# Rotating images by 180 degrees: a last load in two pieces, an earlier release of the first store, and wider copies

## The chip, the cores and the metric

The kernel runs on one core of a Trainium2 chip. Its time is the device time of one execution in microseconds (us); the kernel before takes 122.82 us, the median of three runs (122.74 to 122.94).

## The reference

The input is a batch of images in 32-bit floats, 32 x 3 pictures of 256 x 256. Every picture is turned by 180 degrees, which reverses its rows and the elements of each row:

```python
batch, c, h, w = 32, 3, 256, 256
return np.rot90(x, k=2, axes=(-2, -1)).astype(np.float32)
```

Seen as a flat list of 65,536 elements, a picture is simply reversed. There is no arithmetic: 25.17 MB are read, reordered and written back.

## The kernel before

The 96 pictures make three groups of 32 (G). Each picture is cut into four runs of E = 16,384 elements, so a group is a tile of 128 partitions with one run of 64 KB in each: 8.39 MB. The three groups have a tile of their own, A, Bt and Ct (lines 43 to 45), and all of them fit on the chip at once, beside a small spare tile T of J elements per partition (line 46).

A reversed picture needs its four runs in the opposite order, and each run reversed inside. The two halves of this work are done by different parts of the chip:

- `inside(t)` (line 60) reverses each partition's run in place on the vector engine, DVE. It takes a strip of J elements from the front and the strip of J that mirrors it at the back, and swaps them with three copies (line 52): the back strip reversed into T, the front strip reversed into the back, T into the front. With J = E // 16 = 1024 there are 8 such pairs, thus 24 copies of 128 x 1024 for a tile and 72 in all. They are kept in the order of the program.
- `store(t, g)` (line 58) writes the tile out with the four runs of each picture in the opposite order (`::-1` in the output's access pattern).

All loads (line 55) and stores are issued by the sync engine, SP, whose instructions go in order, and all go into one DMA queue (q1 in the profile) that feeds 16 DMA engines. Each transfer of a whole tile gives every DMA engine eight pieces of 64 KB, one for each of eight partitions, and then a 4-byte write to the transfer's semaphore. The transfer has landed when all 16 engines have done theirs.

SP's program has six transfers: load A, load Bt, load Ct, store A, store Bt, store Ct. The three loads wait for nothing. Store A waits for A to be turned and, by a dependency that is added by hand (line 74), for the last copy on Bt. Store Bt, behind it on SP, needs only the same copy, and store Ct needs the last copy on Ct. At the end SP waits for the landing of the three stores.

The order in the program is:

```python
inside(A)
last = inside(Bt)
first = store(A, 0)      # held back until `last` is done
store(Bt, 1)
inside(Ct)
store(Ct, 2)
```

Of the kernel before, what the change touches and what calls it, by code (L numbers as in the profile page):

```python
# [2 lines left out]

os.environ.setdefault("NEURON_RT_ULTRASERVER_MODE", "4")

# [4 lines left out]


@with_exitstack
def kernel(
    ctx: ExitStack,
    tc: tile.TileContext,
    x: bass.AP,
    out: bass.AP,
):

    nc = tc.nc
    P = 128

    B, C, H, W = x.shape
    L = H * W
    G = 32
    E = L // 4
    J = E // 16

    x4 = x.rearrange("b c h w -> (b c) (h w)").rearrange(
        "(g n) (s e) -> g (n s) e", n=G, s=4)
    o4 = out.rearrange("b c h w -> (b c) (h w)").rearrange(
        "(g n) (s e) -> g n s e", n=G, s=4)  # L40

    pool = ctx.enter_context(tc.tile_pool(name="slots", bufs=1))
    A = pool.tile([P, E], x.dtype, tag="A")
    Bt = pool.tile([P, E], x.dtype, tag="B")
    Ct = pool.tile([P, E], x.dtype, tag="C")
    T = pool.tile([P, J], x.dtype, tag="T")

    def back(t, lo, hi):
        return t[:, hi - 1:(lo - 1 if lo else None):-1]

    def copy(dst, src):
        return tc.keep_in_program_order(nc.vector.tensor_copy(out=dst, in_=src))  # L52

    def load(t, g, lo, hi):
        return nc.sync.dma_start(out=t[:, lo:hi], in_=x4[g][:, lo:hi])  # L55

    def store(t, g):
        return nc.sync.dma_start(out=o4[g][:, ::-1, :], in_=t[:, :])

    def inside(t):  # L60
        for lo in range(0, E // 2, J):
            hi = E - lo - J
            copy(T[:, :], back(t, hi, hi + J))
            copy(t[:, hi:hi + J], back(t, lo, lo + J))
            last = copy(t[:, lo:lo + J], T[:, :])
        return last

    load(A, 0, 0, E)
    load(Bt, 1, 0, E)
    load(Ct, 2, 0, E)  # L70
    inside(A)
    last = inside(Bt)
    first = store(A, 0)
    tc.add_manual_dep(
        first.ins, last.ins.name,
        mybir.DependencyInfo(mybir.DependencyClass.Sync, mybir.DependencyReason.DATA),
        reason="the first store is queued when the second group is turned")
    store(Bt, 1)
    inside(Ct)
    store(Ct, 2)  # L80


# [1 line left out]
_INS = ['x']  # L84
_OUTS = [((32, 3, 256, 256), 'float32')]


# [23 lines left out]
```

## Time and profile before

| what | value |
|---|---|
| time, median of 3 runs | 122.82 us (122.74 to 122.94) |
| profiled execution: its own time, and its span | 122.94 us, 121.16 us |
| bytes read and written | 25.17 MB and 25.17 MB |
| mean rate over the span | 415 GB/s |
| DVE busy | 50.0 us (41% of the span), 72 copies |
| one copy of 128 x 1024 | 694 ns |
| issue to landing: load A, load Bt, load Ct | 22.0, 40.9, 59.8 us |
| issue to landing: store A, store Bt, store Ct | 22.2, 40.8, 41.3 us |

The span is the time from the first to the last instruction on record; the 1.78 us between it and the execution's own time lie around it. "Issue to landing" counts from SP's instruction to the moment that the transfer's semaphore is complete, and so includes the time in which a transfer waits behind others in the queue. The DMA view counts the packets that start in a window; a packet is one piece of a transfer on one DMA engine, and packets under 512 bytes are the writes to semaphores. As a packet's bytes are counted where it starts, the rate in a short window can be far above or below the true one.

### The profile page before, as it was taken

To read this page: it belongs to the slowest core of one execution; us is meant where nothing else is said; L and a number is where in the kernel's file an instruction comes from. 1 tells how busy PE (TensorE), PEld (TensorE's weight loads), DVE (VectorE), ACT (ScalarE), POOL (GpSimd) and SP (SyncE) were. 2 spreads that over 40 slices of the span, in tenths; PEclk is the share of its full clock that TensorE was granted. 3 is DMA by queue.
4 is the path that set the end of the run, shared out by engine and by line. 5 is a ranking of instruction groups with operands and counts; after the bars stand their busy time and mean duration, and the time that the engine had idled before them with its cause. 6 is when DMAs were issued, how large, how long until landed. Compare 5 with 4: busy or idle time off the path is not lost.

```text
span 121.2 us, 126 instructions
## 1 busy us (share of the span) xinstructions
DVE 50.0 (41%) x72; POOL 0.2 (0%) x4
## 2 busy tenths in 40 slices
DVE  0000000499999399999669999900000000000000
POOL 0000000000000000000000000000000000000000
DMA  9778977997889877978898879887988798889880
GB/s 346 346 346 368 671 346 346 389 649 346 346 368 671 346 346 346 692 346 346 346 671 368 349 346 649 368 368 346 649 368 368 346 649 368 368 346 649 368 368 0
DMA packets 865, 50.34 MB, mean 415 GB/s; under 512 B 96, under 2 KB 96, under 8 KB 96
## 3 DMA queue, kind: packets, MB, share of 16 engines
q1 hardware_dynamic: 864, 50.33, 96.7%
q14 instruction: 1, 0.01, 0.0%
HBM read 25.17 MB, written 25.17 MB: 415 GB/s over the span
## 4 chain that ended last, share of the span: by engine, by line
DMA 34%; DVE 28%; another core or an unknown queue 2%; issue 1%; SPq 0%; DVEq 0%
DMA Bt<-in_x_dram 34%; DVE T L52 9%; DVE Ct L52 9%; DVE Bt L52 9%; SPq L55 0%; DVEq L52 0%
## 5 line engine op out<-in xcount | busy, mean ns | idle before, releaser
L52 DVE COPY T<-A 128x1024 f32<-128x1024 f32 x8 | 5.6, 694 | 23.0 <-DMA A<-in_x_dram 22.8
L52 DVE COPY T<-Ct 128x1024 f32<-128x1024 f32 x8 | 5.6, 694 | 2.2 <-DMA Ct<-in_x_dram 2.0
L52 DVE COPY T<-Bt 128x1024 f32<-128x1024 f32 x8 | 5.6, 694 | 2.2 <-DMA Bt<-in_x_dram 2.0
L52 DVE COPY A<-A 128x1024 f32<-128x1024 f32 x8 | 5.6, 694 | 0.3
L52 DVE COPY Ct<-Ct 128x1024 f32<-128x1024 f32 x8 | 5.6, 694 | 0.3
L52 DVE COPY Ct<-T 128x1024 f32<-128x1024 f32 x8 | 5.6, 694 | 0.3
L52 DVE COPY Bt<-T 128x1024 f32<-128x1024 f32 x8 | 5.5, 694 | 0.3
L52 DVE COPY Bt<-Bt 128x1024 f32<-128x1024 f32 x8 | 5.5, 694 | 0.3
L52 DVE COPY A<-T 128x1024 f32<-128x1024 f32 x8 | 5.5, 693 | 0.3
L95 POOL MEMSET const-uint8-127<- 128x1 uint8 x1 | 0.1, 103 | 0.0
L95 POOL MEMSET const-bfloat16-1.0<- 128x1 bf16 x1 | 0.1, 102 | 0.0
L95 POOL MEMSET const-float32-0.0<- 128x1 f32 x1 | 0.1, 99 | 0.2 <-issue 0.2
L95 POOL MEMSET const-float32-1.0<- 128x1 f32 x1 | 0.1, 99 | 0.0
## 6 DMA issues: line engine op xcount, KB each, us to landing
A<-in_x_dram SPq DMA_DIRECT2D x1, 22.0
Bt<-in_x_dram SPq DMA_DIRECT2D x1, 40.9
Ct<-in_x_dram SPq DMA_DIRECT2D x1, 59.8
out_dram<-A SPq DMA_DIRECT2D x1, 22.2
out_dram<-Bt SPq DMA_DIRECT2D x1, 40.8
out_dram<-Ct SPq DMA_DIRECT2D x1, 41.3
```

The lines of the kernel that those rows point to most:

```text
L52: return tc.keep_in_program_order(nc.vector.tensor_copy(out=dst, in_=src))
L95: nc = _bacc.Bacc("TRN2", target_bir_lowering=False, num_devices=1)
```

## The change

Three things are different:

1. The load of Ct is issued as two transfers: the first 14,592 elements of each partition (58,368 bytes, "the body"), and the last TAIL = 1,792 elements (7,168 bytes, "the tail"), which is 0.92 MB over the 128 partitions.
2. Store A no longer waits for the last copy on Bt. By hand it now waits for the landing of the body. Store Bt waits for Bt to be turned, and store Ct for Ct, as each needs. The first copy on Ct waits for both pieces of its load.
3. J is E // 8 = 2048 and not E // 16 = 1024, so that there are 12 copies of 128 x 2048 for a tile, 36 in all, and T has twice the size. The elements that are copied are the same number.

SP's program has seven transfers then, and the order of the transfers in the queue is load A, load Bt, body, tail, store A, store Bt, store Ct.

```diff
-    J = E // 16
+    J = E // 8
...
     def copy(dst, src):
-        return tc.keep_in_program_order(nc.vector.tensor_copy(out=dst, in_=src))
+        tc.keep_in_program_order(nc.vector.tensor_copy(out=dst, in_=src))
...
             copy(T[:, :], back(t, hi, hi + J))
             copy(t[:, hi:hi + J], back(t, lo, lo + J))
-            last = copy(t[:, lo:lo + J], T[:, :])
-        return last
+            copy(t[:, lo:lo + J], T[:, :])
 
+    TAIL = 1792
     load(A, 0, 0, E)
     load(Bt, 1, 0, E)
-    load(Ct, 2, 0, E)
+    body = load(Ct, 2, 0, E - TAIL)
+    load(Ct, 2, E - TAIL, E)
     inside(A)
-    last = inside(Bt)
     first = store(A, 0)
     tc.add_manual_dep(
-        first.ins, last.ins.name,
+        first.ins, body.ins.name,
         mybir.DependencyInfo(mybir.DependencyClass.Sync, mybir.DependencyReason.DATA),
...
-    store(Bt, 1)
-    inside(Ct)
-    store(Ct, 2)
+    for g, t in ((1, Bt), (2, Ct)):
+        inside(t)
+        store(t, g)
```

More of the change, by code (lines that the diff above doesn't have):

```diff
@@ L64, in inside @@
             copy(t[:, hi:hi + J], back(t, lo, lo + J))
-            last = copy(t[:, lo:lo + J], T[:, :])
-        return last
+            copy(t[:, lo:lo + J], T[:, :])
+    TAIL = 1792
     load(A, 0, 0, E)
     load(Bt, 1, 0, E)
-    load(Ct, 2, 0, E)
+    body = load(Ct, 2, 0, E - TAIL)
+    load(Ct, 2, E - TAIL, E)
     inside(A)
-    last = inside(Bt)
     first = store(A, 0)
     tc.add_manual_dep(
-        first.ins, last.ins.name,
+        first.ins, body.ins.name,
         mybir.DependencyInfo(mybir.DependencyClass.Sync, mybir.DependencyReason.DATA),
-        reason="the first store is queued when the second group is turned")
-    store(Bt, 1)
-    inside(Ct)
-    store(Ct, 2)
+        reason="the first store is queued while the last strip is on its way")
+    for g, t in ((1, Bt), (2, Ct)):
+        inside(t)
+        store(t, g)
 _INS = ['x']
```

## The prediction

> **What bounds the kernel now.** I read the page first: its slices of the DMA engines and its queues.
>
> ```profile
> DMA  9778977997889877978898879887988798889880
> q1 hardware_dynamic: 864, 50.33, 96.7%
> q14 instruction: 1, 0.01, 0.0%
> ```
>
> The queue that holds all loads and stores is busy for 96.7% of the span on all 16 engines. DVE (41%) is no bound. In the packet records a 64 KB packet takes 2.418 us and the next starts 2.414 us after it (2.419 us in the stores), so six transfers of eight packets cost an engine at least 48 x 2.414 = 115.9 us of the 121.16 us span. What a change can win is the other 5.3 us: the start, the place where loads give way to stores, and the engines that lag at the end. The page's chain of work is no help here; it stops at the last copy on Ct, some 40 us before the end.
>
> SP's own waits come next, then the timeline round 60 us.
>
> ```profile
> SPq L58 <- DVE Bt L52: 36.8, 1, 36.8
> SPq L106 <- DMA out_dram<-Ct: 19.2, 1, 19.2
> ```
>
> ```profile
> 58.91 0.69 DVE L52 COPY Bt<-T 128x1024 f32<-128x1024 f32 x1
> 59.63 0.63 SPq L58 DMA_DIRECT2D out_dram<-A  x1
> 60.30 0.59 SPq L58 DMA_DIRECT2D out_dram<-Bt  x1
> 61.57 0.70 DVE L52 COPY T<-Ct 128x1024 f32<-128x1024 f32 x1 [1.97 <-DMA Ct<-in_x_dram]
> ```
>
> Store A is issued at 59.63 us, as soon as Bt is turned. Is that early enough to follow the loads without a gap? The DMA view of 60.4 to 60.9 us, then of 60.9 to 61.3 us:
>
> ```profile
> DMA packets 15, 0.00 MB, mean 0 GB/s; under 512 B 15, under 2 KB 15, under 8 KB 15
> ...
> DMA packets 17, 1.05 MB, mean 2621 GB/s; under 512 B 1, under 2 KB 1, under 8 KB 1
> ```
>
> No. Fifteen engines write load Ct's semaphore between 60.54 and 60.84 us, and none has begun a store by 60.9 us. The 16 first packets of store A start from 60.906 us on, 1.28 us and more after the issue. In the packet records the engines stand idle for 0.07 to 0.49 us (mean 0.26 us). The sixteenth engine, 0.35 us behind since the first load, writes its semaphore at 61.18 us and idles for 0.10 us.
>
> The end: the windows 119 to 119.3 us and 119.3 to 120.5 us, and before them 68.5 to 68.9 us.
>
> ```profile
> DMA packets 3, 0.14 MB, mean 348 GB/s; under 512 B 0, under 2 KB 0, under 8 KB 0
> q1 hardware_dynamic: 2, 0.13, 81.1%
> q14 instruction: 1, 0.01, 4.8%
> ```
>
> ```profile
> DMA packets 14, 0.00 MB, mean 0 GB/s; under 512 B 14, under 2 KB 14, under 8 KB 14
> ...
> DMA packets 2, 0.00 MB, mean 0 GB/s; under 512 B 2, under 2 KB 2, under 8 KB 2
> ```
>
> Fourteen engines are done by 119.2 us. The late one of the border ends at 119.47 us, and another at 119.94 us. SP waits for that last one, wakes at 120.37 us, and the span ends 0.8 us later. This last engine was level with the rest at 65.8 us. Then its packet took 2.72 us, an 8 KB packet of the instruction queue (q14) held it for 0.30 us at 68.57 us, and the next took 2.77 us: together 0.95 us behind. So two engines decide the end: one that lost 0.95 us to an instruction fetch, and 0.47 us in front of it one that was late from the start.
>
> **The change part by part.** *Half as many copies.* J = 2048 removes 36 DVE instructions. The trace has no copy of 128x2048; its price lies between 0.694 us (nothing for width) and 1.388 us (twice the row). I take the upper end, as the data doubles. With the 0.034 us that the trace has between copies, a tile takes at most 12 x 1.42 = 17.1 us against 17.5 us. Bt, landed at 42.1 us, is turned by 59.2 us at the latest; store Bt comes behind store A and has 19 us of queue before it, so this hides. Ct is turned by 78.6 us, and store Ct's turn in the queue is at 99.7 us: 21 us of cover. As DVE work this edit is worth 0.
>
> It may do something else: move the fetch. At 68.57 us only DVE is executing; SP waits from 61.5 to 79.0 us, PE, ACT and POOL since 0.8 us. The fetch is DVE's by elimination. DVE was then at its 58th copy, some 63 instructions in. In the changed kernel it has 36 copies and about 42 instructions in all before the last store, so a fetch that comes with the instruction count doesn't occur while data moves. Bounds: 0 (the fetch is not tied to the count) to 0.95 us (all that its engine lost). The end gains only until the next engine decides, 119.94 - 119.47 = 0.47 us. I take 0.47 us.
>
> The Trainium skill ("Runtime: NRT & Kernel Launch", Instruction fetch mechanics) speaks against this: refills are blocks of 256 instructions that the sequencer streams ahead, their cost mostly hidden. The trace has one packet of 8 KB with 72 copies in the program, and an engine that lost 0.95 us beside it. By the page the fetch would be worth nothing, and the sum 122.8 us.
>
> *The release of store A.* It now waits for the body to land; A is turned at 40 us or earlier. The body is 58,368/65,536 of load Ct, so an engine ends it 7,168/65,536 x 19.3 = 2.11 us before it ends the whole load. The late engine counts: 61.18 - 2.11 = 59.07 us, and 0.3 us to landing (61.18 to 61.48 us in the trace) gives 59.37 us. SP's wait and the issue take about 0.09 us (at the start SP passes a wait at 0.65 us and issues at 0.73 us): store A goes out at 59.46 us and not 59.63 us, 0.17 us earlier. So the new wait replaces the old with little difference. At 1.28 to 1.40 us from issue to first packet, packets can start at 60.74 to 60.86 us, while engines finish the tail at 60.54 to 60.84 us. The mean idle falls from 0.26 to about 0.1 us; for the late engine, which decides, from 0.10 us to between 0 and 0.10. I take 0.05 us gained. Behind store A on SP waits only store Bt, issued 0.67 us later as now.
>
> *One more load.* SP issues four, 0.43 us for the fourth at 2.1 us; it hides behind 60 us of queue. DVE's first copy on Ct waits for both pieces, which end when the whole did. The rate of 7 KB pieces is not in the trace. From below: no cost, as the semaphore packets between queued transfers pass without a measurable gap; none can be gained, as the bytes are the same. From above: every new piece starts cold, as load A's first packet does (3.15 us median for 2.42), 0.73 us each and 8 x 0.73 = 5.8 us. The nearest row is the border of load A and load Bt inside a running queue, where 9 semaphore-size packets at 5 ns would be 0.04 us. I take 0.04 us.
>
> The Trainium skill ("DMA: Bandwidth & Descriptors", Anatomy of one DMA) charges each DMA about 2.0 us fixed beside its bytes, and its rules for kernel authors want 1 MiB or more in one DMA; the tail is under that. In the trace loads land 19.3 us apart, their bytes' time and no more. With a fixed 2.0 us exposed the sum would be 124.3 us.
>
> Sum against the profiled execution (122.94 us = span 121.16 + 1.78): -0.47 - 0.05 + 0.04 = -0.48, thus 122.46 us. That execution is 0.12 us above the median of 122.82, to which I apply the difference: 122.34, said as 122.3 us. A measurement of this kernel tells about 0.2% (0.25 us) from no change, so faster means below 122.57 and slower above 123.07 us.
>
> **The rivals.** *The fetch stays, or comes later under the stores* (same). What speaks for it: one packet is thin evidence for a trigger, and the removed instructions may only shift it. Against: DVE alone was running. Then the fetched engine still decides; store A's release gives it at most 0.17 us and the tail takes 0.04: 122.7 us, 122.6 to 122.9.
>
> *Nothing late remains* (faster). If the engine that lags by 0.35 us from its first packet is chance, the end falls to the 14 others: 119.94 - 119.19 = 0.75 us, with 0.17 us of closed gap: 121.9 to 122.0 us. Against: some engine always starts last, and 16 must land.
>
> *The short pieces are slow* (slower). The mechanism is that 7 KB rows don't stay in flight behind each other; place, the tail at 58.6 to 60.7 us; all engines pay. It decides beyond 0.48 + 0.25 = 0.73 us, 0.09 us for each of the eight, which is one cold start for the transfer. Two cold starts, at the tail and behind it, give 122.34 + 1.46 = 123.8 us; one gives 123.07. For it: a piece of this size isn't in the trace. Against: queued pieces show no gap, 4-byte ones included.
>
> **How the numbers follow.** The forecast case, 0.55: 122.1 to 122.55 us. Fetch stays, 0.20: same, except a tenth of it (0.02) at its fast end. Nothing late, 0.08. Short pieces slow, 0.17: 0.13 slower, 0.04 same because the price stays under the point of decision. Faster 0.55 + 0.08 + 0.02 = 0.65, same 0.22, slower 0.13. The range from 122.0 to 122.95 us holds the forecast, most of the fetch rival and the cheap end of the short pieces; outside are some 0.05 below and 0.14 above.
>
> **What the changed profile would show.** No q14 packet in the queues, or one on another place; the windows at the end with 15 engines within 0.2 us and one straggler, not two. Store A issued at 59.4 to 59.5 us and its first packets from 60.75 us. 128 packets of 7,168 bytes, eight of them in 2.1 to 2.2 us on an engine. Copies near 1.2 to 1.4 us. I am wrong if a q14 packet remains inside the stores and the last engine still ends 0.4 us behind, or if the loads end later than 61.3 us.

## The result and the profile after

The changed kernel takes 122.31 us (median of 6 runs, 122.04 to 122.44), the kernel before 122.78 us in the runs beside it. The ratio is 0.9956, with a 95% interval of 0.9941 to 0.9970: 0.47 us or 0.4% faster. Forecast were 122.3 us, and 122.0 to 122.95 us as the range.

The profiled execution of the changed kernel took 122.44 us with a span of 120.7 us, against 122.94 and 121.2 us before. The page's queues after the change (packets, MB, share of 16 engines):

```profile
DMA  9888988898889779799599888988898889888990
...
q1 hardware_dynamic: 1008, 50.33, 97.2%
```

There is no line for the instruction queue q14 any more; before, it had one packet of 8 KB. The 1008 packets are 864 and the 144 of the second piece of load Ct (128 of data, 16 for semaphores).

SP's and DVE's timeline round 60 us, and one row of the page's groups for the price of a copy:

```profile
55.88 1.23 DVE L52 COPY Bt<-T 128x2048 f32<-128x2048 f32 x1
59.63 0.63 SPq L58 DMA_DIRECT2D out_dram<-A  x1
60.36 0.55 SPq L58 DMA_DIRECT2D out_dram<-Bt  x1
61.82 1.23 DVE L52 COPY T<-Ct 128x2048 f32<-128x2048 f32 x1 [4.71 <-DMA Ct<-in_x_dram]
```

```profile
L52 DVE COPY Bt<-Bt 128x2048 f32<-128x2048 f32 x4 | 4.9, 1227 | 0.1
```

Bt is turned at 57.1 us, 2.5 us earlier than before. Store A nevertheless goes out at 59.63 us, to the hundredth as before, because now it waits for the body. The end, in the DMA view of 119 to 119.3 us and of 119.3 to 120.5 us:

```profile
DMA packets 12, 0.00 MB, mean 0 GB/s; under 512 B 12, under 2 KB 12, under 8 KB 12
...
DMA packets 4, 0.00 MB, mean 0 GB/s; under 512 B 4, under 2 KB 4, under 8 KB 4
```

Twelve engines are done before 119.3 us, and four end later, by the packet records from 119.42 to 119.54 us. Before, one engine had ended at 119.94 us. So the last engine ends 0.40 us earlier, while the bulk of the engines ends where it did (the first at 119.04 us before and 119.05 us after; the mean of the 16 at 119.18 and 119.21 us). The gain is at the straggler, as the prediction's main term has it.

### The profile page after: what moved, and what is told of

Read it like the earlier page. It is cut to its first block, busy times and chain, and to the rows that moved or that the text cites. A ratio compares the mean times of both kernels' runs of the same rounds, so it can differ in the third digit from the quotient of the medians.

```text
span 120.7 us, 93 instructions
## 1 busy us (share of the span) xinstructions
DVE 44.2 (37%) x36; POOL 0.2 (0%) x4
## 2 busy tenths in 40 slices
DMA packets 1008, 50.33 MB, mean 417 GB/s; under 512 B 112, under 2 KB 112, under 8 KB 240
## 3 DMA queue, kind: packets, MB, share of 16 engines
q1 hardware_dynamic: 1008, 50.33, 97.2%
## 4 chain that ended last, share of the span: by engine, by line
DMA 34%; DVE 25%; another core or an unknown queue 4%; issue 1%; SPq 0%; DVEq 0%
DMA Bt<-in_x_dram 34%; DVE T L52 8%; DVE Bt L52 8%; DVE Ct L52 8%; SPq L55 0%; DVEq L52 0%
## 5 line engine op out<-in xcount | busy, mean ns | idle before, releaser
L52 DVE COPY T<-A 128x2048 f32<-128x2048 f32 x4 | 4.9, 1227 | 22.7 <-DMA A<-in_x_dram 22.6
L52 DVE COPY T<-Ct 128x2048 f32<-128x2048 f32 x4 | 4.9, 1228 | 4.8 <-DMA Ct<-in_x_dram 4.7
L52 DVE COPY T<-Bt 128x2048 f32<-128x2048 f32 x4 | 4.9, 1226 | 4.4 <-DMA Bt<-in_x_dram 4.3
L52 DVE COPY Bt<-T 128x2048 f32<-128x2048 f32 x4 | 4.9, 1228 | 0.1
L52 DVE COPY Ct<-Ct 128x2048 f32<-128x2048 f32 x4 | 4.9, 1228 | 0.1
L52 DVE COPY A<-T 128x2048 f32<-128x2048 f32 x4 | 4.9, 1227 | 0.1
L52 DVE COPY Bt<-Bt 128x2048 f32<-128x2048 f32 x4 | 4.9, 1227 | 0.1
L52 DVE COPY Ct<-T 128x2048 f32<-128x2048 f32 x4 | 4.9, 1227 | 0.1
L52 DVE COPY A<-A 128x2048 f32<-128x2048 f32 x4 | 4.9, 1226 | 0.1
## 6 DMA issues: line engine op xcount, KB each, us to landing
Ct<-in_x_dram SPq DMA_DIRECT2D x1, 7296.0 KB, 57.9
```

## The experiments

Three sets of runs, each with runs of the kernel before on the same chip. Where a ratio is given, it is to those, with its 95% interval.

**Which part brings the gain?** The first run makes only the copies wider; the second does everything but that.

```diff
-    J = E // 16      # in the kernel before
+    J = E // 8
```

> The kernel before with J = E // 8 alone: one load of Ct, store A held until Bt is turned. Theory (the gain is the instruction fetch that no longer occurs): no packet of the instruction queue (q14) under the stores, and Bt turned at about 57.2 us, so that store A is issued 2.4 us earlier than before and the idle of the engines between loads and stores (mean 0.26 us) closes too: 122.0 to 122.3 us. Rival (the gain came from the split load and the new release): no gain, 122.7 to 122.9 us.

Measured: 122.36 us, ratio 0.9964 (0.9951 to 0.9976), no q14 packet. The interval overlaps that of the whole change, so the wider copies alone bring what can be told of the gain. One part of the expectation failed: the border did not get cheaper. Store A was issued at 57.26 us and the engines had no idle between loads and stores, but each engine's last packet of load Ct took 0.56 us longer than 2.418 us (mean over the 16, from the packet records).

```profile
57.26 0.63 SPq L58 DMA_DIRECT2D out_dram<-A  x1
```

Even so the mean engine ended at 119.16 us (119.18 before), because the idle was gone and its stores were shorter (57.95 us from the first packet to the last semaphore, 58.20 before). The last engine ended at 119.53 us and not 119.94.

```diff
-    J = E // 8       # in the changed kernel
+    J = E // 16
```

> The changed kernel with J = E // 16 again: split load of Ct, store A released by the body, 72 copies of 128x1024. Theory (the fetch): the q14 packet is back in the stores, one engine ends some 0.5 us behind the next, 122.6 to 122.9 us. Rival (the release made the gain): 122.2 to 122.4 us with the q14 packet or without.

Measured: 122.93 us (122.66 to 123.43), ratio 1.0009 (0.9996 to 1.0022), with a q14 packet of 8 KB at 68.36 us, which the DMA view of 68 to 68.6 us has:

```profile
q14 instruction: 1, 0.01, 3.2%
```

The median is 0.03 us above the theory's range; of the twelve runs, eight lie between 122.66 and 122.96 us and four between 123.10 and 123.43 us. The split load and the new release are worth nothing that can be told from zero by themselves. In its profile one engine wrote its last semaphore at 119.73 us and the next at 119.16 us.

**Is it the fetch, and does it follow the instruction count?** Two runs give DVE instructions back (36, and in the second run 30), as copies of 128x8 that it has time for, and leave the 128x2048 copies as they are.

```diff
+    def extra(n):
+        for _ in range(n):
+            copy(S[:, :], T[:, 0:8])       # S: a new tile of 128x8
+
     inside(A)
+    extra(18)
...
         inside(t)
+        if g == 1:
+            extra(18)
         store(t, g)
```

> The changed kernel with 36 additional copies of 128x8 on DVE, 18 behind A and 18 behind Bt, in DVE's idle time; the number of DVE instructions is that of the kernel before. Theory (the fetch comes with DVE's instruction count): a q14 packet of 8 KB is back, when DVE is at about its 58th copy, that is in the first copies on Ct at 64 to 68 us; one engine loses some 0.9 us there, and the time goes back to 122.6 to 122.9 us. Rival (the fetch belongs to something else, such as the elapsed time or the narrow copies): no q14 packet, 122.2 to 122.4 us.

Measured: the q14 packet is back, so the fetch does come with the number of DVE's instructions. DVE's timeline and the DMA view of 60.4 to 60.9 us:

```profile
57.32 3.67 DVE L53 COPY S<-T 128x8 f32<-128x8 f32 x18
```

```profile
q14 instruction: 1, 0.01, 3.9%
```

It came at 60.51 us, while DVE was near the end of the extra copies, at its 58th copy in all, as in the kernel before; the expectation had put the place wrong because the extra copies bring the count up earlier. The time did not go back to 122.7 us: the median is 122.45 us, ratio 0.9981 (0.9964 to 0.9999), with nine runs from 122.15 to 122.54 and three from 123.07 to 123.47 us, a scatter that I can't explain. In the profiled run (122.41 us) the fetch came at the border between loads and stores, when five of the 16 engines had ended load Ct. No 7 KB piece took longer for it (0.272 us, as all the others); one 64 KB packet of store A, begun 0.05 us after the fetch had ended, took 2.80 us where the others took 2.46 to 2.48 us. That engine ended at 119.20 us, ahead of the last one at 119.48 us, so the fetch did not set the end. The next run moves the fetch to where it was.

```diff
     inside(A)
-    extra(18)
+    extra(10)
...
-            extra(18)
+            extra(20)
```

> The changed kernel with 30 additional copies of 128x8, 10 behind A and 20 behind Bt. In the run with 18 and 18 the q14 packet came back at 60.5 us, at DVE's 62nd or 63rd instruction and while the 7 KB pieces were on their way, and its engine lost little. Here the 63rd instruction is the fourth copy on Ct, about 65.5 us, under the 64 KB packets of store A. Theory (a fetch costs its engine 0.9 us where it falls among 64 KB packets): q14 packet at 65 to 68 us, one engine 0.6 to 1.0 us behind from there on, 122.7 to 122.9 us. Rival (the fetch is harmless and the engine's lag had another cause): q14 packet, no new lag, 122.2 to 122.45 us.

Measured: 122.87 us, ratio 0.9995 (0.9986 to 1.0003). The changed kernel itself, on the same chip and in the same set:

> The changed kernel once more on the chip of these runs, to compare them with it: 122.1 to 122.4 us.

Measured: 122.35 us, ratio 0.9953 (0.9941 to 0.9965). The two differ by 30 tiny copies in DVE's idle time, and by 122.87 - 122.35 = 0.52 us: the whole gain is gone. That the copies themselves cost this is unlikely, as the run before had 36 of them and nine of its runs at 122.15 to 122.54 us. The fetch came at 68.60 us, a little later than the expectation had it, on DVE's 60th copy. The DMA view of the run with the fetch, from 68 to 69 us, and at its end from 118.7 to 119.35 and from 119.35 to 120.5 us:

```profile
DMA packets 13, 0.79 MB, mean 795 GB/s; under 512 B 0, under 2 KB 0, under 8 KB 0
q1 hardware_dynamic: 12, 0.79, 184.0%
q14 instruction: 1, 0.01, 1.9%
```

```profile
DMA packets 15, 0.00 MB, mean 0 GB/s; under 512 B 15, under 2 KB 15, under 8 KB 15
...
DMA packets 1, 0.00 MB, mean 0 GB/s; under 512 B 1, under 2 KB 1, under 8 KB 1
```

Fifteen engines end within 119.3 us and one alone at 119.97 us, 0.68 us behind the next; it was 0.80 us behind at the end of store A, the transfer in which the fetch fell. The rival that the fetch is harmless is out. The Trainium skill's "Runtime: NRT & Kernel Launch" (Instruction fetch mechanics) calls the cost of instruction refills mostly hidden. Here it is 0.5 us of the kernel's time, because SP waits for the slowest of 16 engines.

**What is the release good for?** If the border's idle came only from the late issue, store A should simply be issued as early as possible.

```diff
     load(A, 0, 0, E)
     load(Bt, 1, 0, E)
-    body = load(Ct, 2, 0, E - TAIL)
-    load(Ct, 2, E - TAIL, E)
-    inside(A)
-    first = store(A, 0)
-    tc.add_manual_dep(...)
-    for g, t in ((1, Bt), (2, Ct)):
+    load(Ct, 2, 0, E)
+    for g, t in ((0, A), (1, Bt), (2, Ct)):
         inside(t)
         store(t, g)
```

> J = E // 8, one load of Ct, and no wait by hand: store A is issued when A is turned, about 38 us, behind the loads in the queue. Theory (idle at the border is only the 1.28 us from issue to first packet): no idle between loads and stores, no q14 packet, 121.9 to 122.2 us. Rival (a store that is queued early disturbs the loads that are still running): load Ct lands later than 61.3 us and the time is 122.5 us or more.

Measured: 122.99 us, ratio 1.0009 (1.0000 to 1.0017), without any fetch. What the missing fetch gives is lost again. The DMA view of this run from 60.4 to 61.4 us, and from 61.4 to 62.3 us:

```profile
DMA packets 0, 0.00 MB, mean 0 GB/s; under 512 B 0, under 2 KB 0, under 8 KB 0
...
DMA packets 32, 1.05 MB, mean 1165 GB/s; under 512 B 16, under 2 KB 16, under 8 KB 16
```

In the kernel before, 15 of 16 engines had finished load Ct by 60.9 us. Here not one has by 61.4 us. Then all 16 write the semaphore and start store A at once, with no idle (0.002 us on average in the packet records). Each engine's last packet of load Ct, begun at about 58.2 us as before, took 3.56 us on average and not 2.42 us. So an early store removes 0.26 us of idle and adds 1.14 us to the loads in front of it: the rival was right. Does the loss shrink with the piece in front of the store?

```diff
     body = load(Ct, 2, 0, E - TAIL)      # changed kernel: split load kept,
     load(Ct, 2, E - TAIL, E)
-    inside(A)                            # but no wait by hand
-    first = store(A, 0)
-    tc.add_manual_dep(...)
-    for g, t in ((1, Bt), (2, Ct)):
+    for g, t in ((0, A), (1, Bt), (2, Ct)):
```

> The changed kernel without the wait by hand: body and tail of 7 KB, store A issued when A is turned (37.7 us). With one load of Ct and no wait, each engine's last 64 KB packet of the load took 1.14 us longer. Theory (a queued store slows only the packet of the load that is directly in front of it, in proportion to its size): the last 7 KB piece loses 0.12 us, no idle at the border, 122.0 to 122.3 us. Rival (the queued store costs the loads the same 1.1 us whatever the size of the last piece): 122.9 to 123.2 us.

Measured: 123.23 us, ratio 1.0027 (1.0012 to 1.0042), 0.03 us above the rival's range. My theory falls. The loss is 1.2 us again, spread over the 7 KB pieces: those begun between 58.2 and 61.2 us took up to 0.78 us longer than the 0.26 us of their bytes, and the last two, directly in front of the store, lost next to nothing. The loss is about the same whatever the size of the last piece; it falls in the last 3 us or so before the store's data.

That leaves the moment of release. Three tails release store A at different times:

```diff
-    TAIL = 1792      # 7 KB of each row
+    TAIL = 2304      # 9 KB; then 2816 (11 KB) and 3584 (14 KB)
```

> The changed kernel with TAIL = 2304 (9,216 bytes): the body lands 0.6 us earlier, so store A is issued at 58.8 to 59.0 us. Theory (the border's idle is the late issue): first store packets follow the loads without idle (0.26 us mean idle gone), 122.0 to 122.25 us. Rival (the last pieces of the load are slowed instead, as with one load and an early store): idle gone but the load's end later by as much, 122.3 us or more.

> The changed kernel with TAIL = 2816 (11,264 bytes). The body lands 1.2 us earlier than with 7 KB, so store A is issued at 58.2 us and could start at 59.5 us, 1.1 us ahead of the loads' end. So far a store that could start 0.3 us ahead cost the loads nothing (9 KB), 1.9 us ahead 0.56 us (one load, wide copies), and much earlier 1.1 us. Theory (the cost to the loads grows with the time that the store waits behind them): 0.1 to 0.4 us lost in the last pieces, 122.2 to 122.5 us. Rival (only a store that comes before the last 64 KB or 2.4 us costs anything): as with 9 KB, 122.0 to 122.2 us.

> The changed kernel with TAIL = 3584 (14,336 bytes): store A issued at 57.4 us, able to start 1.9 us ahead of the loads' end, as in the run with one load and wide copies. Theory (cost by lead time, not by the size of the last piece): the last pieces lose about 0.5 us per engine, 122.4 to 122.7 us. Rival (small pieces shield the load at this lead): 122.0 to 122.2 us.

| tail | store A issued (profile) | loss in load Ct beyond its bytes, mean per engine | start of store A's packets, mean, behind the ideal | time, ratio |
|---|---|---|---|---|
| 7 KB (repeat) | 59.45 us | 0.07 us | 0.24 us | 122.35 us, 0.9953 (0.9941 to 0.9965) |
| 9 KB | 58.78 us | 0.07 us | 0.12 us | 122.10 us, 0.9935 (0.9922 to 0.9948) |
| 11 KB | 58.10 us | 0.17 us | 0.15 us | 122.36 us, 0.9963 (0.9950 to 0.9977) |
| 14 KB | 57.50 us | 0.48 us | 0.51 us | 122.41 us, 0.9965 (0.9952 to 0.9979) |
| one load, wide copies | 57.26 us | 0.56 us | 0.56 us | 122.36 us, 0.9964 (0.9951 to 0.9976) |
| one load, no wait | 37.65 us | 1.15 us | 1.15 us | 122.99 us, 1.0009 (1.0000 to 1.0017) |

The loss and the start are worked out from the packet records: the time that packets of load Ct took beyond 2.418 us for 64 KB, and the first packets of store A against load Ct's first packets plus 8 x 2.415 = 19.32 us. Each row's first three figures are from one profile, and each ratio is to the kernel before on the same chip; the first two rows share a chip.

One thing the table leaves out: where the stores follow the loads without any idle (the last four rows, and the 7 KB tail without the wait), the mean engine takes 57.95 us from its first store packet to its last semaphore. In the rows of 7 and 9 KB it takes 58.15 and 58.13 us, and 58.16 us in the changed kernel. So these runs get back 0.18 to 0.2 us in the stores of what they lose in the loads. Why, no run here shows.

With 9 KB the timeline and the end (119 to 119.5 us) read:

```profile
58.78 0.63 SPq L58 DMA_DIRECT2D out_dram<-A  x1
59.50 0.55 SPq L58 DMA_DIRECT2D out_dram<-Bt  x1
61.56 1.23 DVE L52 COPY T<-Ct 128x2048 f32<-128x2048 f32 x1 [4.32 <-DMA Ct<-in_x_dram]
```

```profile
DMA packets 5, 0.00 MB, mean 0 GB/s; under 512 B 5, under 2 KB 5, under 8 KB 5
```

Store A comes 0.67 us earlier than with 7 KB in the same set, the engines start it 0.08 us after the end of their loads on average (0.19 us with 7 KB), and the last engine ends at 119.28 us. At 122.10 us (122.09 to 122.18 in five runs) this has the lowest median here; on that chip the kernel before took 122.89 us. Its interval still overlaps that of the 7 KB kernel (0.9941 to 0.9965) by a little, and two runs of the 7 KB kernel in the result's set took 122.04 and 122.06 us, so that 9 KB is faster than 7 KB is likely but not shown. The 11 KB run shows that the mean is not all: its engines are on average the earliest to end (118.73 us against 118.85 us with 9 KB), but two of them lagged from load Ct on and ended at 119.21 and 119.35 us. The 14 KB run met neither of its two theories: its profile shows 0.13 us lost in the tail's pieces (0.06 us with 7 KB), where the theory had 0.5, and 0.36 us in the body, 41 to 48 us, long before any store was queued.

## Why the prediction was right, and where it was not

- **The bound and the end.** Right. The gain is 0.40 us at the last engine between the two profiles, while the first engine to end does so at 119.04 and 119.05 us. What was read from 14 and 2 semaphore packets at the end was the thing to read.
- **Half as many copies move the fetch: 0.47 us.** Right in cause and size. The fetch is gone with 36 copies, comes back with the instruction count alone, and costs 0.52 us when it falls into the stores as before. "By elimination" was a sound argument, and the trigger was confirmed: the fetch came during DVE's 58th copy in the kernel before, in the run with 1024-wide copies and in the run with 18 and 18 extra copies, and during its 60th in the run with 10 and 20; with 36 copies in all no profile has one. What the prediction did not see is that the place matters: at the border between loads and stores one packet took 0.32 us longer, and that engine was not the last. That the size came out so close is in part luck. The 0.47 us is the lead of the last engine over one that in that trace was late since the first load; in the profile after, four other engines that fell behind in load Ct happened to end within 0.1 us of the same time.
- **The copy's price, 0.694 to 1.388 us, worth 0.** Right: 1.227 us, and hidden. But "turned earlier" is not harmless in itself: with one load and the old wait, the wider copies release store A at 57.26 us, and the loads pay 0.56 us for it.
- **The release of store A: issue at 59.46 us, 0.05 us gained.** The prediction's idle of 0.07 to 0.49 us for single engines is one way to pair the records, which don't name the engine; paired in the order of time they give about 0.1 to 0.4 us, and only the mean of 0.26 us is sure. The issue time holds in the repeat of the changed kernel (body landed at 59.36 us, issue at 59.45 us). In the profiled run of the result it failed: four engines fell behind in the body (their semaphores at 59.04 to 59.20 us, the other twelve by 58.79 us), it landed at 59.54 us, and the store went out at 59.63 us. The term was for one late engine that the trace of before had; which engines are late, and by how much, changes from run to run. The split and release alone had no measurable gain, which fits 0.05 us and equally 0.
- **The tail costs 0.04 us.** Nearly right: the records have 0.272 us for a 7 KB piece whose bytes take 0.264 us, 8 x 0.008 = 0.06 us. No cold start showed, so the slower rival was wrong. The 2.0 us that the prediction quotes from the Trainium skill ("DMA: Bandwidth & Descriptors", Anatomy of one DMA) is a figure for DMAs issued from GpSimd. The tail was issued by SP and queued behind another transfer, and 0.06 us was all that it cost.
- **The end after: one straggler.** There were four, at 119.42 to 119.54 us; the time of the last (119.46 us worked out: 119.47 - 0.05 + 0.04) was right to 0.1 us.
- **What would have made the prediction wrong and was not in it:** a store that is queued early slows the loads. Nothing in the trace of before shows it, as its store is issued only 1.1 us before most engines finish. Had the change released store A with A itself, my working would have promised 0.26 us of closed idle; the run that does this lost 1.2 us in the loads and 123.23 - 122.35 = 0.88 us in the kernel's time.

## What to carry to other kernels

When one transfer engine of 16 sets the end, look at who is last and why, not at the mean: here 0.5 us hung on a single 8 KB packet of the instruction queue, and fewer, larger instructions removed it. Release a store so that it just follows the loads: at the border between loads and stores a little too late cost 0.26 us of idle, much too early 1.1 us of slower loads, of which 0.2 us came back in the stores. Count an instruction fetch by the engine's instruction number and see which transfers run at that moment.

## What was not expected of the hardware

- A store in the queue behind a load slowed the load's last 3 us: by 1.15 us per engine when it was issued 23 us before the loads' unhindered end (60.7 us), by 0.56 us when issued 3.4 us before, by about 0.1 us when issued 3.2 us (14 KB tail) or 2.6 us before (11 KB), and by nothing when issued 1.9 us before (9 KB). With the earliest issue the loss was 1.15 and 1.19 us with a last piece of 64 KB and of 7 KB. Whether the size of the pieces matters between 3.2 and 3.4 us, and which resource the two share, is open. So is which store does it: with store A issued at 37.65 us the loads lost about 0.01 us per engine between 41 and 57.9 us, and the slow packets began only after store Bt too had been issued, at 57.04 us. No run holds back store Bt alone.
- An instruction fetch of 8 KB, 0.31 us long by its own record, put its engine 0.8 to 0.95 us behind among 64 KB packets, since the packets next to it took 0.30 and 0.35 us longer too.
- In some runs engines lost 0.2 to 0.7 us in the first packets of load Ct, between 41 and 50 us: about five of 16 in the profile of the result, eight in that of the fetch among the stores, most in that of the 14 KB tail, none with 9 KB or in the repeat of the changed kernel. What causes this is open too; it is as large as what the sizes of the tail were to tell apart.
